# A streaming encoder layer on one core: another order of the products in the input projection, and weight sums of the up projection kept in DRAM

## The chip, the core and the metric

The kernel runs on one core of a Trainium2 chip. A core has five engines that each work through their own queue of instructions in order: TensorE (PE in the profile; it loads a stationary operand, PEld, and streams a moving one through it), VectorE (DVE), ScalarE (ACT), GpSimd (POOL) and SyncE (SP, which here only issues DMAs). They wait for one another by semaphores. Matrix products accumulate in PSUM banks, everything else lies in SBUF, and 16 DMA engines move data between SBUF and DRAM. The metric is the device time of one execution in microseconds (us).

## The reference

One layer over 2048 prompt frames and 8 x 16 sample frames (2176 columns together), model width 1024, in float32:

```
h = rms_norm(x, g_mix_pre)
qa, ka, va, qb, kb, vb, ga, gb = split(h @ w_in)        # w_in: 1024 x 4352
qa, ka = rope(qa), rope(ka)
oa = sliding-window attention with sinks (qa, ka, va)
ob = chunk-band attention with relative bias (qb, kb, vb)
mixed = sigmoid(ga) * (oa @ w_oa) + sigmoid(gb) * (ob @ w_ob)
x = x + rms_norm(mixed @ w_out, g_mix_post)
u, val = split(rms_norm(x, g_ffn_pre) @ w_up)           # w_up: 1024 x 5632
conv = conv_b + causal depthwise convolution of u, 3 taps
x = x + rms_norm((gelu(conv) * val) @ w_down, g_ffn_post)
```

The outputs are x of both parts, new rows of the caches, and the last two rows of u.

## The kernel before

The stages follow one another: input projection (to about 860 us), attention (to 1500), output projection (to 1757), up projection (to 2763), down projection. The change touches the first and the fourth.

**A float32 product from three.** Every operand is split into a high part (`hi`, a cast on ACT, L143) and the rest (`lo`, a subtraction on DVE, L144), and `mm3` runs three matmuls for each 128 rows of depth: hi by xhi (L138), hi by xlo (L139), lo by xhi (L140).

**Seven products for eight.** Two output tiles of 128 rows and two column ranges of n columns are made together from seven products instead of eight (the Strassen-Winograd form), each of 4 x 3 matmuls; the sums of weights and of inputs that it needs are made beforehand. `seven` issues the products in the order of a table of (product, bank), three PSUM banks in all: products 1 and 2 add up in bank 0; 6, 7 and 4 in bank 1; 5 and 3 in bank 2. Banks are read between the products: s1 is a copy of bank 0 after product 1 (ACT), q is bank 1 + s1 after product 6 (DVE), and product 7 adds to bank 1 only when q has been read; t is bank 1 + s1 after product 7, and product 4 waits for that; product 2 waits for s1.

**Input projection.** After four output tiles that are made directly come 41 "pairs" of tiles: 15 in a first block of columns, 17 in a second (n = 384 in both), 9 in a third (n = 320). In the first two blocks, pairs of queries, keys and values take turns with pairs of gates. Queries and keys get a rotary step on ACT and DVE (L331 to L352) and go to DRAM as hi and lo. For a pair, `in_place` loads two raw weight tiles (`wraw`, `wrow`, 512 KB each), splits `wraw` (products 1 and 2) and half of `wrow` (`whib`, `wlob`: product 4), lets POOL make four sums in the same tiles (L257 to L260), and splits the sums: `wrow` for products 7 and 5, `wraw` again as `whic`, `wloc` for products 6 and 3. It is called for the next pair before the present one is issued.

**Up projection.** Three blocks of columns, 22 units each (66 in all; n = 364, 364, 360). `stationary` loads two raw tiles per unit, POOL writes four sums to a tile `ws` (one buffer; L193 to L196), and they are split like the others. `up` runs the seven products (order 1, 6, 5, 7, 2, 4, 3), then the convolution, the gelu and the product, and stores `gd` (L1229). At the start of a block, `moving` makes the sums and splits of the block's x: DVE (L1081, L1083), POOL (L1087, L1090), and seven splits `x1h`, `x1l` and so on.

**What sets the order.** The code states what depends on what; a list scheduler, which estimates when each operation can run, then sets the order of instructions in each engine's queue. An operation that is issued earlier in the program has the higher priority. An instruction that waits holds up all that is behind it on its engine.

Of the kernel before, what the change touches and what calls it, by code (L numbers as in the profile page):

```python
# [10 lines left out]
F32 = mybir.dt.float32  # L11
# [6 lines left out]
P = 128  # L18
# [8 lines left out]
NF = FF // P  # L27
# [26 lines left out]
ORDER = ((1, 0), (6, 1), (5, 2), (7, 1), (2, 0), (4, 1), (3, 2))  # L54

IBLOCKS = [(0, 384), (768, 384), (1536, 320)]
IORDER = ((1, 0), (5, 2), (6, 1), (7, 1), (2, 0), (4, 1), (3, 2))
IW = 384
DIRECT = 4
LATES = ((1536, 320), (1856, 320))  # L60
# [37 lines left out]
def encoder_layer(ctx: ExitStack, tc: tile.TileContext, i, o):  # L98
# [17 lines left out]
    md = [dram.tile([P, T], F32, name=f"md{p}") for p in range(8)]  # L116
    xd = [dram.tile([P, T], F32, name=f"xd{p}") for p in range(8)]
    extd = dram.tile([8, NT, EXT], F32, name="extd")
    gd = [dram.tile([P, T], F32, name=f"gd{f}") for f in range(NF)]


# [60 lines left out]
    wp = Weights(ctx.enter_context(tc.tile_pool(name="wraw", bufs=2)),  # L182
                 ctx.enter_context(tc.tile_pool(name="whl", bufs=3)))

    def stationary(src0, src1, wx, sx):

        r0 = wp.raw.tile([P, 8, P], F32, name="wraw")
        r1 = wp.raw.tile([P, 8, P], F32, name="wraw")
        dma(out=r0, in_=src0)
        dma(out=r1, in_=src1)  # L190
        sums = sx.tile([P, 16, P], F32, name="ws")
        s1, s2, s3, s4 = [sums[:, 4 * z:4 * z + 4] for z in range(4)]
        G.tensor_add(out=s1, in0=r1[:, 0:4], in1=r1[:, 4:8])  # L193
        G.tensor_sub(out=s2, in0=s1, in1=r0[:, 0:4])  # L194
        G.tensor_sub(out=s3, in0=r0[:, 0:4], in1=r1[:, 0:4])  # L195
        G.tensor_sub(out=s4, in0=r0[:, 4:8], in1=s2)  # L196
        w = {}

        def put(pool, tag, src, names):
            nk = 4 * len(names)  # L200
            hi = pool.tile([P, nk, P], F32R, name=f"whi{tag}", tag=f"whi{tag}")
            lo = pool.tile([P, nk, P], F32R, name=f"wlo{tag}", tag=f"wlo{tag}")
            split(hi, lo, src)
            for z, name in enumerate(names):
                w[name] = (hi[:, 4 * z:4 * z + 4], lo[:, 4 * z:4 * z + 4])

        put(wp.hl, "", r0, (1, 2))
        put(wx, "b", r1[:, 4:8], (4,))
        put(wp.hl, "", sums[:, 0:8], (5, 6))
        put(wx, "c", sums[:, 8:16], (7, 3))  # L210
        return w

    def seven(w, x, n, evac, bank_pool, order):

        ps = [bank_pool.tile([P, 512], F32, name="psm3")[:, :n] for _ in range(3)]
        began = set()
        for z, (name, bank) in enumerate(order):
            (whi, wlo), (xhi, xlo) = w[name], x[name]
            for k in range(4):
                mm3(ps[bank], whi[:, k], wlo[:, k], xhi[:, k], xlo[:, k],  # L220
                    k == 0 and bank not in began, k == 3, bank in began)
            began.add(bank)
            evac(z, ps)
# [4 lines left out]
    with ExitStack() as ph:  # L228
# [9 lines left out]
        def in_place(src0, src1):  # L238

            r0 = wp.raw.tile([P, 8, P], F32, name="wraw")  # L240
            r1 = wr.tile([P, 8, P], F32, name="wrow")
            dma(out=r0, in_=src0)
            dma(out=r1, in_=src1)
            a11, a12, a21, a22 = r0[:, 0:4], r0[:, 4:8], r1[:, 0:4], r1[:, 4:8]
            w = {}

            def put(pool, tag, src, names):
                nk = 4 * len(names)
                hi = pool.tile([P, nk, P], F32R, name=f"whi{tag}", tag=f"whi{tag}")
                lo = pool.tile([P, nk, P], F32R, name=f"wlo{tag}", tag=f"wlo{tag}")  # L250
                split(hi, lo, src)
                for z, name in enumerate(names):
                    w[name] = (hi[:, 4 * z:4 * z + 4], lo[:, 4 * z:4 * z + 4])

            put(wp.hl, "", r0, (1, 2))
            put(wx, "b", a22, (4,))
            G.tensor_add(out=a22, in0=a21, in1=a22)  # L257
            G.tensor_sub(out=a21, in0=a11, in1=a21)
            G.tensor_sub(out=a11, in0=a22, in1=a11)
            G.tensor_sub(out=a12, in0=a12, in1=a11)  # L260
            put(wp.hl, "", r1, (7, 5))
            put(wx, "c", r0, (6, 3))
            return w

        def segments(t0, n):

# [182 lines left out]
            put(3, b22)  # L449
            yield x  # L450

        def pair(u, bi, w, x):
            b0, n = IBLOCKS[bi]
            ta, tb = b0, b0 + n
            s1, q, t = [ev.tile([P, IW], F32, name=z)[:, :n] for z in ("s1", "q", "t")]

            def tile_f():
                return ev.tile([P, IW], F32, name="f", bufs=4)[:, :n]

            def ready(z, ps):  # L460
                if z == 0:
                    S.copy(out=s1, in_=ps[0])  # L462
                elif z == 2:
                    V.tensor_add(out=q, in0=ps[1], in1=s1)
                elif z == 3:
                    V.tensor_add(out=t, in0=ps[1], in1=s1)  # L466
                    f = tile_f()
                    V.tensor_add(out=f, in0=ps[2], in1=t)
                    evac(u + 1, tb, n, f)
                elif z == 4:  # L470
                    f = tile_f()
                    S.copy(out=f, in_=ps[0])
                    evac(u, ta, n, f)
                elif z == 5:
                    f = tile_f()
                    V.tensor_add(out=f, in0=ps[1], in1=s1)
                    evac(u + 1, ta, n, f)
                elif z == 6:
                    f = tile_f()
                    V.tensor_add(out=f, in0=ps[2], in1=q)  # L480
                    evac(u, tb, n, f)

            seven(w, x, n, ready, psm, IORDER)

        hp2 = [None]

# [66 lines left out]
            units += [(bi, u) for u in turns]  # L553
        weights = lambda u: in_place(i["w1"][u], i["w1"][u + 1])
        ws = [weights(units[0][1])]
        for x in xgen:
            pass
        nxt = iter(())
        seen = 0
        for z, (bi, u) in enumerate(units):  # L560
# [14 lines left out]
                nxt = iter(())  # L575
            if z + 1 < len(units):
                ws.append(weights(units[z + 1][1]))
            if bi < 2 and u == 20:
                nxt = stage(bi + 1)
            hs = next(nxt, hs)  # L580
            pair(u, bi, ws.pop(0), x)
        late.update({g: (x[y], x[y2]) for g, y, y2 in ((0, 1, 2), (1, 0, 3))})
    xr.close()

# [589 lines left out]
    with ExitStack() as ph:  # L1174
# [11 lines left out]
        def up(bi, f, w, x):  # L1186
# [21 lines left out]
                elif z == 6:  # L1208
                    V.tensor_add(out=u1, in0=ps[2], in1=q)

            seven(w, x, n, evac, psm, ORDER)
            cv = sp.tile([P, NBK], F32, name="cv", bufs=2)[:, :nb]
            S.activation(out=cv, in_=ue[:, 2:2 + nb], func=AF.Identity, bias=cw[:, f, 3:4], scale=cw[:, f, 2:3])
            V.tensor_copy(out=hist[:, f], in_=ue[:, npr:npr + 2])
# [14 lines left out]
            dma(out=gd[f][:, b0:b0 + nb], in_=cv)  # L1229

        units = [(bi, f) for bi in range(3) for f in range(NF)]
        ws = [stationary(i["wu"][f], i["wu"][NF + f], wx, sx) for _, f in units[:1]]
        x = None
        for z, (bi, f) in enumerate(units):
            if f == 0:
                if bi:
                    xgen = moving(hs, SBLOCKS[bi][1], hq, lambda: hx)
                for x in xgen:
                    pass
            if z + 1 < len(units):  # L1240
                g = units[z + 1][1]
                ws.append(stationary(i["wu"][g], i["wu"][NF + g], wx, sx))
            if f == 16 and bi < 2:
                hs = stage(bi + 1)
            up(bi, f, ws.pop(0), x)
# [149 lines left out]
```

## Time and profile before

| | us |
|---|---|
| median of 3 runs (lowest, highest) | 3318.76 (3317.17, 3323.16) |
| profiled execution, whole | 3322.67 |
| profiled execution, span of the trace | 3320.6 |
| PE, DVE, ACT, POOL busy | 3069.1, 2187.1, 1483.7, 776.4 |
| input projection, 50 to 840 us: PE waits for q, for s1 | 39.7, 27.4 |
| up projection, busy time of POOL's four sums (66 units) | 92.9 + 112.1 + 95.5 + 127.1 |

The profile is of one execution, so the rows below have one duration for each instruction. Busy time of PE includes matmuls at either level of its clock (1.2 and 2.4 GHz); PEclk is the mean granted clock of a window as a share of the upper one. The idle time before an instruction stands in brackets with what released it. Names are those of the program, without buffer numbers (`s` is s1, `psm` a PSUM bank of a pair or unit).

### The profile page before, as it was taken

Reading aid. Unit: us, or ns where it says so; the run is one execution under the profiler, and the core shown is the slowest. Engines: PE = TensorE matmul, PEld = TensorE weight load, DVE = VectorE, ACT = ScalarE, POOL = GpSimd, SP = SyncE. Lnnn points to the kernel's source line nnn. Section 1 sums busy time; section 2 is a strip of 40 time slices with the busy share of each in tenths; the row PEclk is TensorE's granted clock in tenths of the full one; section 3 lists DMA queues with packets and bytes.
Section 4 is the critical chain, followed back from the end, with each engine's and each line's share of the span. In section 5 each row is a group of like instructions: output and inputs, shape, how many; then the busy total and the mean of one; then the engine's idle time right before and its main releaser. Section 6 shows DMA issues by size and latency. Waiting matters only on the chain.

```text
span 3320.6 us, 49296 instructions
## 1 busy us (share of the span) xinstructions
PE 3069.1 (92%) x18188; PEld 2833.1 (85%) x18188; DVE 2187.1 (66%) x3632; ACT 1483.7 (45%) x2647; POOL 776.4 (23%) x612
## 2 busy tenths in 40 slices
PE   6888898977799999999997999899989999999997
PEld 5788788876787777789996999799989998888897
DVE  7755657456347766554688877987787775445445
ACT  5544445344238766313444444444444444433432
POOL 2233432332111111000003444444444440000000
PEclk8999999988999999999998999999999999999999
DMA  4543445435676663674534222322222226556554
GB/s 137 167 139 110 136 130 149 137 97 157 201 249 193 178 166 113 199 223 155 162 115 140 98 97 103 117 103 97 100 85 101 103 98 204 168 163 201 158 177 148
DMA packets 276666, 479.14 MB, mean 144 GB/s; under 512 B 33729, under 2 KB 171337, under 8 KB 276425
## 3 DMA queue, kind: packets, MB, share of 16 engines
q1 hardware_dynamic: 272328, 462.36, 45.0%
q0 software_dynamic: 4096, 13.64, 1.2%
q8 instruction: 143, 2.34, 0.3%
q14 instruction: 99, 0.80, 0.1%
HBM read 360.71 MB, written 115.15 MB: 143 GB/s over the span
## 4 chain that ended last, share of the span: by engine, by line
PE 57%; DVE 8%; POOL 5%; issue 3%; ACT 2%; DMA 2%; SPq 0%; POOLq 0%; DVEq 0%; ACTq 0%
PE psm L138 14%; PE psm L140 14%; PE psm L139 14%; PE pso L908 4%; PE pst L925 3%; PE pss L863 2%; DVE wlo L144 2%; POOL ws L194 1%; DVE cv L1216 1%; POOL ws L196 1%; POOL ws L193 1%; PE pss L839 1%; POOL ws L195 1%; ACT whi L143 1%; PE psf L138 1%
## 5 line engine op out<-in xcount | busy, mean ns | idle before, releaser
L144 DVE TENSOR_TENSOR wlo<-wraw,whi 128x1024 fp32r<-128x1024 f32 (+1 forms) x259 | 346.5, 1339 | 374.9 <-ACT whi L143 371.4
L143 ACT CAST whi<-wraw 128x1024 fp32r<-128x1024 f32 (+1 forms) x259 | 263.2, 1017 | 547.8 <-PE psm L139 452.8
L138 PE MATMUL psm<-ghl,whi 128*128 128x464 f32 (+1 forms) x880 | 320.4, 364 | 2.7 <-ACT ghl L143 2.2
L139 PE MATMUL psm<-ghl,whi 128*128 128x464 f32 (+1 forms) x880 | 317.7, 361 | 2.0 <-DVE ghl L144 2.0
L140 PE MATMUL psm<-ghl,wlo 128*128 128x464 f32 (+1 forms) x880 | 317.0, 360 | 1.0 <-DVE wlo L144 1.0
L193 POOL TENSOR_TENSOR ws<-wraw 128x512 f32<-128x512 f32 x66 | 92.9, 1407 | 566.3 <-DVE wlo L144 449.0
L138 PEld LDWEIGHTS psm<-ghl,whi 128*128 128x128 f32 x880 | 165.8, 189 | 20.9 <-ACT ghl L143 3.3
L140 PEld LDWEIGHTS psm<-ghl,wlo 128*128 128x128 f32 x880 | 165.9, 189 | 18.4 <-DVE wlo L144 1.6
L139 PEld LDWEIGHTS psm<-ghl,whi 128*128 128x128 f32 x880 | 166.3, 189 | 18.0 <-DVE ghl L144 2.8
L138 PE MATMUL psm<-x2h,whi 128*128 128x364 f32 (+3 forms) x428 | 150.3, 351 | 33.6 <-ACT s L462 30.4
L138 PE MATMUL psm<-x5h,whi 128*128 128x364 f32 (+3 forms) x428 | 144.4, 337 | 26.1 <-ACT whi L143 9.8
L257 POOL TENSOR_TENSOR wrow<-wrow 128x512 f32<-128x512 f32 x41 | 57.9, 1412 | 469.1 <-DVE wlob L144 436.4
L138 PE MATMUL psm<-x4h,whib 128*128 128x364 f32 (+3 forms) x428 | 145.1, 339 | 18.6 <-DVE t L466 12.3
L138 PE MATMUL psm<-x3h,whic 128*128 128x364 f32 (+3 forms) x428 | 143.0, 334 | 10.1 <-DVE vv L1203 7.2
L139 PE MATMUL psm<-x2l,whi 128*128 128x364 f32 (+3 forms) x428 | 147.3, 344 | 4.1 <-DVE x2l L144 4.1
L138 PE MATMUL psm<-mhi,whi 128*128 128x272 f32 x512 | 150.7, 294 | 0.0
L140 PE MATMUL psm<-mhi,wlo 128*128 128x272 f32 x512 | 148.1, 289 | 0.0
L139 PE MATMUL psm<-mlo,whi 128*128 128x272 f32 x512 | 147.5, 288 | 0.0
L138 PE MATMUL psm<-x1h,whi 128*128 128x364 f32 (+3 forms) x428 | 144.2, 337 | 2.8 <-ACT x1h L143 1.3
L140 PE MATMUL psm<-x2h,wlo 128*128 128x364 f32 (+3 forms) x428 | 146.1, 341 | 0.0
L139 PE MATMUL psm<-x5l,whi 128*128 128x364 f32 (+3 forms) x428 | 143.0, 334 | 2.5 <-DVE x5l L144 2.5
L140 PE MATMUL psm<-x1h,wlo 128*128 128x364 f32 (+3 forms) x428 | 143.8, 336 | 1.7 <-DVE wlo L144 1.7
(368 smaller groups left out, 9599.1 us busy)
## 6 DMA issues: line engine op xcount, KB each, us to landing
wraw<-in_wu SPq DMA_DIRECT2D x132, 512.0 KB, 4.1
wraw<-in_wd SPq DMA_DIRECT2D x80, 512.0 KB, 3.7
wraw<-in_w SPq DMA_DIRECT2D x69, 512.0 KB, 3.8
wrow<-in_w SPq DMA_DIRECT2D x41, 512.0 KB, 3.9
keys<-kd SPq DMA_DIRECT2D x80, 256.0 KB, 4.3
gx<-gd SPq DMA_DIRECT2D x88, 232.0 KB, 4.0
q<-qd SPq DMA_DIRECT2D x64, 256.0 KB, 4.2
gd<-cv SPq DMA_DIRECT2D x44, 364.0 KB, 2.3
```

The source lines that it names most:

```text
L138: TE.matmul(ps, lhsT=hi, rhs=xhi, start=first, stop=False, skip_group_check=more)
L139: TE.matmul(ps, lhsT=hi, rhs=xlo, start=False, stop=False, skip_group_check=more)
L140: TE.matmul(ps, lhsT=lo, rhs=xhi, start=False, stop=last, skip_group_check=more)
L143: S.copy(out=hi, in_=src)
L144: E.tensor_sub(out=lo, in0=src, in1=hi.bitcast(F32))
L193: G.tensor_add(out=s1, in0=r1[:, 0:4], in1=r1[:, 4:8])
L194: G.tensor_sub(out=s2, in0=s1, in1=r0[:, 0:4])
L195: G.tensor_sub(out=s3, in0=r0[:, 0:4], in1=r1[:, 0:4])
L257: G.tensor_add(out=a22, in0=a21, in1=a22)
L863: TE.matmul(ps[:, off + n0:off + n1], lhsT=q[:, j * P:(j + 1) * P], rhs=keys[hf][:, z, k0 + n0:k0 + n1], start=(z == 0), stop=(z == 1))
L908: TE.matmul(ps_o[hf * HD:(hf + 1) * HD, q0 * P:(q0 + nq) * P], lhsT=v[:, hf * HD:(hf + 1) * HD], rhs=tsb[hf][:, col:col + nq * P], start=( ...
L925: TE.transpose(out=tp[:, col:col + P], in_=u["P"][hf][j][:, bl * P:(bl + 1) * P], identity=ident)
```

## The change

Three edits. The input projection takes its products in the table `ORDER`, as the up projection does: 1, 6, 5, 7, 2, 4, 3 instead of 1, 5, 6, 7, 2, 4, 3, and q is taken after the second product. `in_place` becomes a generator: its first part (loads, first splits, sums) runs before the pair as it did, its last two splits are issued within the pair after its fifth product. In the up projection, block 1 also stores the tile of sums to DRAM (`sd`, 1 MB for each of 22 units); blocks 2 and 3 load it instead of making it, and load only half of the second raw tile.

```diff
-IORDER = ((1, 0), (5, 2), (6, 1), (7, 1), (2, 0), (4, 1), (3, 2))
...
+    sd = [dram.tile([P, 16, P], F32, name=f"sd{f}") for f in range(NF)]
...
-    def stationary(src0, src1, wx, sx):
+    def stationary(src0, src1, wx, sx, kept, first):
...
-        dma(out=r1, in_=src1)
+        if first:
+            dma(out=r1, in_=src1)
+        else:
+            dma(out=r1[:, 4:8], in_=src1[:, 4:8])
         sums = sx.tile([P, 16, P], F32, name="ws")
-        s1, s2, s3, s4 = [sums[:, 4 * z:4 * z + 4] for z in range(4)]
-        G.tensor_add(out=s1, in0=r1[:, 0:4], in1=r1[:, 4:8])
-        G.tensor_sub(out=s2, in0=s1, in1=r0[:, 0:4])
-        G.tensor_sub(out=s3, in0=r0[:, 0:4], in1=r1[:, 0:4])
-        G.tensor_sub(out=s4, in0=r0[:, 4:8], in1=s2)
+        if first:
+            s1, s2, s3, s4 = [sums[:, 4 * z:4 * z + 4] for z in range(4)]
+            G.tensor_add(out=s1, in0=r1[:, 0:4], in1=r1[:, 4:8])
+            G.tensor_sub(out=s2, in0=s1, in1=r0[:, 0:4])
+            G.tensor_sub(out=s3, in0=r0[:, 0:4], in1=r1[:, 0:4])
+            G.tensor_sub(out=s4, in0=r0[:, 4:8], in1=s2)
+            dma(out=kept, in_=sums)
+        else:
+            dma(out=sums, in_=kept)
...
-    def seven(w, x, n, evac, bank_pool, order):
+    def seven(w, x, n, evac, bank_pool):
...
-        for z, (name, bank) in enumerate(order):
+        for z, (name, bank) in enumerate(ORDER):
...
             G.tensor_sub(out=a12, in0=a12, in1=a11)
+            yield w
             put(wp.hl, "", r1, (7, 5))
             put(wx, "c", r0, (6, 3))
-            return w
+            yield w
...
-        def pair(u, bi, w, x):
+        def pair(u, bi, w, x, ahead):
...
-                elif z == 2:
+                elif z == 1:
                     V.tensor_add(out=q, in0=ps[1], in1=s1)
...
                     S.copy(out=f, in_=ps[0])
+                    next(ahead, 0)
                     evac(u, ta, n, f)
...
         ws = [weights(units[0][1])]
+        w = next(ws[0])
+        next(ws[0])
...
                 ws.append(weights(units[z + 1][1]))
+                nw = next(ws[-1])
...
-            pair(u, bi, ws.pop(0), x)
+            pair(u, bi, w, x, ws[-1])
+            w = nw
...
-                ws.append(stationary(i["wu"][g], i["wu"][NF + g], wx, sx))
+                ws.append(stationary(i["wu"][g], i["wu"][NF + g], wx, sx, sd[g], units[z + 1][0] == 0))
```

What the scheduler makes of it is shown at three places. PE first, in pair 6 of the first block (pairs counted from 0). Before, from the end of product 6 (`x6h`) over the beginning of product 2 (`x2h`) to the beginning of product 7 (`x7h`):

```order
L139 MATMUL psm_1893<-x6l,whic 128x384
L140 MATMUL psm_1893<-x6h,wloc 128x384
L138 MATMUL psm_1892<-x2h,whi 128x384
L139 MATMUL psm_1892<-x2l,whi 128x384
L140 MATMUL psm_1892<-x2h,wlo 128x384
L138 MATMUL psm_1892<-x2h,whi 128x384
L139 MATMUL psm_1892<-x2l,whi 128x384
L138 MATMUL psm_1893<-x7h,whi 128x384
L139 MATMUL psm_1893<-x7l,whi 128x384
```

After, from the end of product 5 (`x5h`), which now follows product 6, to the beginning of product 7:

```order
L138 MATMUL psm_1908<-x5h,whi 128x384
L139 MATMUL psm_1908<-x5l,whi 128x384
L140 MATMUL psm_1908<-x5h,wlo 128x384
L138 MATMUL psm_1907<-x7h,whi 128x384
L139 MATMUL psm_1907<-x7l,whi 128x384
L140 MATMUL psm_1907<-x7h,wlo 128x384
L138 MATMUL psm_1907<-x7h,whi 128x384
```

Five matmuls of product 2 stood between product 6 and product 7; now all of product 5 stands there, and product 2 follows product 7.

DVE in the same pair. `psm_1893` before and `psm_1907` after are bank 1 of the pair; `wloc` belongs to the next pair's weights. Before:

```order
L144 TENSOR_TENSOR wlob<-wrow,whib 128x512
L352 SCALAR_TENSOR_TENSOR lo<-f,hi 128x384
L480 TENSOR_TENSOR f<-psm_1756,q 128x384
L144 TENSOR_TENSOR wloc<-wraw,whic 128x1024
L464 TENSOR_TENSOR q<-psm_1893,s_1889 128x384
L466 TENSOR_TENSOR t<-psm_1893,s_1889 128x384
L468 TENSOR_TENSOR f<-psm_1894,t 128x384
```

After (q is now L472, t is L474, f L476):

```order
L360 SCALAR_TENSOR_TENSOR lo<-f,hi 128x384
L144 TENSOR_TENSOR wlob<-wrow,whib 128x512
L489 TENSOR_TENSOR f<-psm_1770,q 128x384
L472 TENSOR_TENSOR q<-psm_1907,s_1903 128x384
L144 TENSOR_TENSOR wloc<-wraw,whic 128x1024
L474 TENSOR_TENSOR t<-psm_1907,s_1903 128x384
L476 TENSOR_TENSOR f<-psm_1908,t 128x384
```

q and `wloc` have changed places here. Over the 40 pairs that have a next one, q now stands ahead of the next pair's `wloc` in 14 (1 to 6, 12, 15, 16, 22, 24, 25, 35 and 36) and behind it in 26; before it stood behind it in about 34.

POOL at the start of block 2 of the up projection, whose sums for x are L1087 and L1090 before and L1100 and L1103 after. Before:

```order
L196 TENSOR_TENSOR ws<-wraw,ws 128x512
L1087 TENSOR_TENSOR hst<-hst 128x4x364
L193 TENSOR_TENSOR ws<-wraw 128x512
L195 TENSOR_TENSOR ws<-wraw 128x512
L194 TENSOR_TENSOR ws<-ws,wraw 128x512
L196 TENSOR_TENSOR ws<-wraw,ws 128x512
L1090 TENSOR_TENSOR xt<-hst,xt 128x1456
L193 TENSOR_TENSOR ws<-wraw 128x512
```

After, from the last weight sums of block 1 over the starts of blocks 2 and 3:

```order
L197 TENSOR_TENSOR ws<-wraw 128x512
L199 TENSOR_TENSOR ws<-wraw 128x512
L198 TENSOR_TENSOR ws<-ws,wraw 128x512
L200 TENSOR_TENSOR ws<-wraw,ws 128x512
L1100 TENSOR_TENSOR hst<-hst 128x4x364
L1103 TENSOR_TENSOR xt<-hst,xt 128x1456
L1100 TENSOR_TENSOR hst<-hst 128x4x360
L1103 TENSOR_TENSOR xt<-hst,xt 128x4x360
```

Four weight sums stood between the two x sums of a block; after the change POOL has nothing but the x sums in blocks 2 and 3.

## Rows read from the trace of the kernel before

**Rows 1.** The page's first part: busy us, share of the span, instructions.

```profile
PE 3069.1 (92%) x18188; PEld 2833.1 (85%) x18188; DVE 2187.1 (66%) x3632; ACT 1483.7 (45%) x2647; POOL 776.4 (23%) x612
```

**Rows 2.** Busy time by windows; last three columns: clock, DMA share, GB/s.

```profile
52.00:215.00 163.00, 124.86 (x610) 118.36 (x609) 109.33 (x138) 81.72 (x123) 55.98 (x36) 0.86 0.50 142
2095.00:2187.00 92.00, 76.22 (x422) 72.92 (x421) 83.85 (x89) 38.98 (x47) 45.67 (x22) 0.94 0.31 110
2187.00:2430.00 243.00, 242.74 (x1450) 242.44 (x1450) 194.65 (x242) 110.19 (x139) 102.31 (x69) 1.00 0.28 102
2430.00:2519.00 89.00, 76.12 (x427) 73.06 (x426) 75.63 (x100) 38.14 (x47) 44.79 (x24) 0.94 0.22 81
```

**Rows 3.** Waits of PE, 50 to 840 us: total, times, longest, in us.

```profile
PE psm L138 <- DVE q L464: 39.7, 29, 4.8
PE psm L138 <- ACT s L462: 27.4, 23, 2.9
```

**Rows 4.** Timeline, pairs 0 and 6: start, duration, engine, [idle before, releaser].

```profile
87.60 0.55 DVE L464 TENSOR_TENSOR q<-psm,s 128x384 f32<-128x384 f32 x1
200.28 0.34 PE L139 MATMUL psm<-x2l,whi 128*128 128x384 f32 x1
201.43 1.04 ACT L143 CAST whic<-wraw 128x1024 fp32r<-128x1024 f32 x1 [4.58 <-POOL wraw L260]
202.51 1.23 DVE L144 TENSOR_TENSOR wloc<-wraw,whic 128x1024 fp32r<-128x1024 f32 x1 [4.31 <-ACT whic L143]
203.65 0.55 DVE L464 TENSOR_TENSOR q<-psm,s 128x384 f32<-128x384 f32 x1
204.26 0.44 PE L138 MATMUL psm<-x7h,whi 128*128 128x384 f32 x1 [3.64 <-DVE q L464]
205.57 0.52 PE L138 MATMUL psm<-x7h,whi 128*128 128x384 f32 x1
```

**Rows 5.** Timeline, a later pair of block 1, at the same place.

```profile
444.10 0.33 PE L139 MATMUL psm<-x6l,whic 128*128 128x384 f32 x1
444.27 0.34 PE L140 MATMUL psm<-x6h,wloc 128*128 128x384 f32 x1
444.30 1.23 DVE L144 TENSOR_TENSOR wloc<-wraw,whic 128x1024 fp32r<-128x1024 f32 x1 [5.34 <-ACT whic L143]
445.44 0.55 DVE L464 TENSOR_TENSOR q<-psm,s 128x384 f32<-128x384 f32 x1
446.05 0.44 PE L138 MATMUL psm<-x7h,whi 128*128 128x384 f32 x1 [0.21 <-DVE q L464]
```

**Rows 6.** Timeline at the start of block 2 of the up projection.

```profile
2097.76 4.25 POOL L1087 TENSOR_TENSOR hst<-hst 128x1456 f32<-128x1456 f32 x1 [8.77 <-DVE hst L1081]
2099.18 4.36 DVE L1083 TENSOR_TENSOR xt<-hst 128x1456 f32<-128x1456 f32 x1
2106.58 2.32 DVE L144 TENSOR_TENSOR x6l<-xt,x6h 128x1456 fp32r<-128x1456 f32 x1
2112.70 3.26 POOL L1090 TENSOR_TENSOR xt<-hst,xt 128x1456 f32<-128x1456 f32 x1
2115.99 1.41 ACT L143 CAST x4h<-xt 128x1456 fp32r<-128x1456 f32 x1 [5.56 <-POOL xt L1090]
2119.34 0.67 PE L138 MATMUL psm<-x6h,whi 128*128 128x364 f32 x1 [6.12 <-ACT whi L143]
```

**Rows 7.** Timeline: POOL in a steady unit of block 2, stores of block 3.

```profile
2315.66 1.30 POOL L193 TENSOR_TENSOR ws<-wraw 128x512 f32<-128x512 f32 x1 [8.04 <-DVE wlo L144]
2319.54 2.15 POOL L196 TENSOR_TENSOR ws<-wraw,ws 128x512 f32<-128x512 f32 x1
2529.86 0.33 SPq L1229 DMA_DIRECT2D gd<-cv  x1
2742.80 0.33 SPq L1229 DMA_DIRECT2D gd<-cv  x1
```

**Rows 8.** The page's DMA issues: count, KB each, median us to landing.

```profile
wraw<-in_wu SPq DMA_DIRECT2D x132, 512.0 KB, 4.1
```

More of the change, by code (lines that the diff above doesn't have):

```diff
@@ L481, in ready @@
                     evac(u, tb, n, f)
-            seven(w, x, n, ready, psm, IORDER)
+            seven(w, x, n, ready, psm)
         hp2 = [None]
@@ L1209, in evac @@
                     V.tensor_add(out=u1, in0=ps[2], in1=q)
-            seven(w, x, n, evac, psm, ORDER)
+            seven(w, x, n, evac, psm)
             cv = sp.tile([P, NBK], F32, name="cv", bufs=2)[:, :nb]
@@ L1231, in encoder_layer @@
         units = [(bi, f) for bi in range(3) for f in range(NF)]
-        ws = [stationary(i["wu"][f], i["wu"][NF + f], wx, sx) for _, f in units[:1]]
+        ws = [stationary(i["wu"][f], i["wu"][NF + f], wx, sx, sd[f], True) for _, f in units[:1]]
         x = None
```

## The prediction

> **What bounds the kernel now.** I began with the engines' shares: TensorE (PE) is busy for 92% of the span, VectorE (DVE) for 66%, ScalarE (ACT) for 45%, GpSimd (POOL) for 23% [rows 1]. So the change can only pay where PE stands still or runs at the lower clock, and the busy time by windows says where that is. In the middle of the up projection's block 2 PE is busy 242.74 of 243 us at a clock of 1.00; at the starts of its blocks 2 and 3 it is idle for 15.8 of 92 us and 12.9 of 89 us; in the first pairs of the input projection it is busy 124.86 of 163 us at a mean clock of 0.86 [rows 2]. POOL sums taken from the steady up units free an engine that bounds nothing there; they count at the block starts.
>
> The waits of PE in the input projection come next: two waits lead, on q (39.7 us, 29 times) and on s (27.4 us, 23 times) [rows 3]. The timeline shows why both are late. Queues are in order, and the next pair's weights stand in front: ACT's cast `whic` waits for POOL's sums, DVE's `wloc` waits for `whic`, and DVE's q waits behind `wloc`. In an early pair, `whic` starts at 201.43, `wloc` runs from 202.51, q from 203.65, and PE, which had started its last matmul at 200.28, goes on at 204.26 after 3.64 us of nothing; then its matmuls last 0.52 us, where they took 0.34 before: the clock has dropped from 2.4 to 1.2 GHz [rows 4]. In a later pair the same queue costs less: product 6 starts its last matmul at 444.27, q starts at 445.44, product 7 at 446.05 [rows 5].
>
> **Part one: order of the products.** Before, PE runs 1, 5, 6, then five matmuls of 2, then 7. After, it runs 1, 6, 5, 7, 2, 4, 3. At full clock a matmul takes 0.17 us (444.10 to 444.27 [rows 5]), a product of twelve 2.08 us and a pair of 84 14.5 us. q now has product 5 as cover, 2.08 us, but loses the five matmuls of 2, 0.87 us, and it is needed 2.08 us earlier counted from product 1. So the change helps where q can be issued on time, and hurts where q still stands behind `wloc`.
>
> The changed order on DVE decides which. q now stands ahead of `wloc` in pairs 1 to 6 of block 0 and in eight later ones (counting pairs from 0), and still behind it in 26 of 40.
>
> Pairs 1 to 6: from q of pair 0 at 87.60 to q of pair 6 at 203.65 are six pairs of 19.3 us [rows 4], 4.8 over the 14.5 of pure matmuls. The q wait goes, and with it the half-clock stretch behind it. But I do not give back all 4.8: DVE is busy for 109.33 of the 163 us [rows 2], that is 15 us for each of the 7.3 pairs' worth of matmuls recorded there (610/84), so the splits, the rotary steps and their stores become late next. I take 16.5 us a pair: 6 x 2.8 = 17 us. Bounds: 0 (evacuation bounds these pairs at 19.3 anyway) and 6 x 4.8 = 29.
>
> The eight later pairs with q in front: of the 67.1 us of q and s waits [rows 3], about 20 lie in pairs 1 to 6 (up to 3.64 each [rows 4]). The other 47 spread over 34 pairs; eight of them at the mean have 11 us, and with a little half clock behind the longest I take 12 (bounds 5 and 20).
>
> The pairs still blocked: q is ready when `wloc` is done, whatever PE does in between. In [rows 5] PE was ready for product 7 at 444.27 + 0.17 = 444.44, and it began at 446.05: 1.6 us, of which five matmuls of 2 filled 0.87. After the change nothing fills it, and those five run later. 26 pairs are in this case by the order, 7 of which lie near block starts or the tail, where PE waits for other things anyway; 19 x 0.87 = 16.5, I take a loss of 16 us. Bounds: a loss of 26 x 0.87 = 23, and 0, because the late issue of the splits also puts s ahead of `whic` more often (before, `whic` came first in 24 of 40 pairs, after in 16 to 18).
>
> The late issue itself (the splits `put` after product 2) adds no instruction; it moves priorities, and its effect is the order just counted. SP's loads for a pair stay ahead of it. Input projection: -17 - 12 + 16 = -13 us.
>
> **Part two: sums kept in DRAM.** Of 66 x 4 POOL sums, 44 x 4 go. In exchange block 1 writes 22 x 1 MB, and blocks 2 and 3 read 44 x 1 MB less the 44 x 0.25 MB of the second row that is left out: 33 MB more.
>
> *Block starts.* At the start of block 2, POOL does its first stage sum at 2097.76, then four weight sums, then the second stage sum from 2112.70 to 2115.96; `x4h` on ACT waits for that until 2115.99; two casts later PE resumes at 2119.34, after 6.12 us of nothing [rows 6]. Block 3 does the same. After the change POOL's two stage sums stand next to each other, 10.7 us sooner. What is late next is DVE: splits of the new x (2.32 us each here, beside POOL [rows 6]). The two windows hold 15.8 + 12.9 = 28.7 us of idle PE [rows 2]; I take half, 14 us. Bounds: 0 (DVE's splits bound it alone) and 29.
>
> Here the trace has DVE's L1083 at 4.36 us, begun while POOL's L1087 (4.25 us) was running, and ended 1.5 us after it [rows 6]. The Trainium skill, SBUF — State Buffer, "Who interferes with whom", says that a DVE instruction with two SBUF inputs and a GpSimd instruction that reads SBUF share a port, and that the later one is blocked for the whole of the first. The trace agrees. By that rule L1083 stays at about 4.4 us, since L1087 stays beside it, and the 2 us that PE waits behind it stay too; had the weight sums been what slows it, the term would be 14 + 2 x 2.3 = 18.6. The half that I take needs neither.
>
> *Block 3's steady units.* The stores of gd at 2529.86 and 2742.80 are 15 units apart: 14.20 us each. Scaled by 360/364 columns from the 0.1674 us of a matmul in block 2 (242.74/1450 [rows 2]) a unit of 84 is 13.91 us [rows 7]. I put the 0.29 us down to q behind `wloc`, as in the input projection; without POOL's sums in front `whic` can start sooner. 15 x 0.29 = 4 us gained, bounds 0 and 6.
>
> *Is the load of the sums on time?* The buffer `ws` is free when POOL starts its next sums, 2315.66, and they end at 2319.54 + 2.15 = 2321.69 [rows 7]. A load issued at 2315.6 has 6.1 us to be no later. Two raw loads of 512 KB, issued together, land in 4.1 us [rows 8], so 1 MB should land at about 2319.8. I cost it at 0; bounds below.
>
> *Block 1.* The write of `ws` holds the only `ws` buffer until it has landed, and stands in SP's queue before the next unit's loads. By the same 4.1 us it ends well inside a unit of 14 us, but at the block's start, where loads pile up, I take a loss of 3 us (bounds 0, and 22 x 1 = 22 if each write puts one raw load late by 1 us).
>
> Up projection: -14 - 4 + 3 = -15 us.
>
> **Sum.** -13 - 15 = -28 us. The profiled execution took 3322.67 us, 2.1 over its span, and 3.9 over the median of the runs, 3318.76; no term hangs on that difference, so I take the sum from the median: 3318.76 - 28 = 3291 us.
>
> **Rivals.**
> *Slower: stalls that bring the clock down.* The still blocked pairs stall for 1.6 us with nothing in between. After 3.64 us the clock fell [rows 4]. The 1.6 us of [rows 5] were half filled by matmuls of 2 and say nothing of an empty stall of that length. If it brings the clock down, product 7 runs at 1.2 GHz, 12 x 0.16 = 1.9 us more. Over 19 pairs this is +36, so 3327; over all 26, with their extra 0.87 for the other seven, +55, so 3346. Middle 3336. Against it: a stall must repeat at this size, and many are shorter. Chance 0.10.
> *Slower or even: late loads.* PE is never late on these sums in block 2 (242.74 of 243 us [rows 2]), so the load decides from a landing somewhat over 6.1 us after its issue; from there each us is paid in up to 42 units, and 1 us past it the time is 3291 + 42 = 3333. For it: it queues behind the gd store and in one queue with the raw loads. Against: the DMA engines are busy only 28% of that stretch [rows 2]. Chance 0.04.
> *No change.* Evacuation keeps pairs 1 to 6 at 19.3 (0 instead of -17), the other stage-1 terms cancel (-12 + 16), and the block starts give only a third: 3318.76 + 4 - 10 + 3 - 4 = 3312; with block starts giving nothing, 3322. Between them, about 3317. Chance 0.14.
> *Better.* Pairs 1 to 6 reach 15 us (-26), blocked pairs lose nothing, block starts give 24: -26 - 12 - 24 - 4 + 3 = -63: 3256. Chance 0.12.
> *My forecast*, 0.60, with its own range 3273 to 3308.
>
> **The numbers.** Range 3260 to 3319: the lower end takes in nearly all of the forecast and most of the better case; the upper end takes half of the no-change case and leaves out the two slower ones (0.14). Runs can tell about 0.2%, 6.6 us. Faster than 3312.1: 0.60 + 0.12 + 0.05 = 0.77. Within: 0.09, nearly all from the no-change case. Slower: 0.14.
>
> **What would show it.** In the changed profile: the q wait of the input projection well under 39.7 us in pairs 1 to 6 and their spacing 16 to 17 us; the s wait smaller; q waits of 1 to 1.7 us in pairs like that of [rows 5] with the clock after them at 0.34 us a matmul (at 0.52 the first rival holds); POOL without weight sums at the starts of blocks 2 and 3 and no 6-us wait on `x4h`; a unit of 13.9 to 14.0 us in block 3. I am wrong if pairs 1 to 6 stay near 19 us, if a wait for the load of `ws` appears in blocks 2 and 3, or if the clock of the input projection falls below what it is now.

## The result and the profile after

The changed kernel takes 3294.72 us in the median of 4 runs (3290.96 to 3296.18), the kernel before 3317.97 us on the same chip (4 runs): a ratio of 0.9929, 95% interval 0.9910 to 0.9948, so 0.7% faster. The forecast was 3291 us. The profiled executions differ by more than the medians, 3292.1 against 3320.6 us of span; the parts below are read from these two and add up to 28.5 us, not to the 23 of the medians.

First the page's busy times, as in [rows 1]:

```profile
PE 3049.7 (93%) x18188; PEld 2829.8 (86%) x18188; DVE 2121.1 (64%) x3632; ACT 1484.0 (45%) x2645; POOL 489.9 (15%) x436
```

POOL has lost 286.5 us, ten times what the span has: that engine bounded nothing over most of it. PE's own busy time is 19 us less for the same 18188 matmuls, which points to fewer of them at the lower clock.

Where the time went, by one event at each place (q is its start on DVE, the end of a unit is the start of its last matmul, of product 3; both read from the timelines of the two kernels):

| point | before | after | difference |
|---|---|---|---|
| q of pair 6 | 203.65 | 186.88 | -16.8 |
| q of the last pair (40) | 846.59 | 833.84 | -12.8 |
| up projection, unit 0 ends | 1793.64 | 1782.53 | -11.1 |
| unit 20 (late in block 1) | 2088.38 | 2086.97 | -1.4 |
| unit 25 (block 2 has started) | 2180.47 | 2168.04 | -12.4 |
| unit 42 | 2419.49 | 2406.87 | -12.6 |
| unit 47 (block 3 has started) | 2507.94 | 2488.00 | -19.9 |
| unit 65, the last | 2763.12 | 2737.00 | -26.1 |
| end of the span | 3320.6 | 3292.1 | -28.5 |

So the early pairs win 16.8 us and the other pairs give 4.0 back; block 1 of the up projection gives 9.7 back; the starts of blocks 2 and 3 win 11.0 and 7.3; block 3's units win 6.2. Of block 1's 9.7 us, 2.9 are lost by unit 4 and 6.8 in the steady units 4 to 20.

The windows that answer to [rows 2] (each begins and ends at the same work as there; columns as there):

```profile
52.00:198.00 146.00, 112.54 (x606) 108.09 (x605) 107.90 (x138) 81.32 (x123) 53.90 (x36) 0.92 0.57 157
2093.00:2175.00 82.00, 75.21 (x428) 74.02 (x427) 72.91 (x89) 40.25 (x47) 7.59 (x2) 0.96 0.49 171
2187.00:2406.00 219.00, 219.00 (x1310) 219.00 (x1309) 152.25 (x217) 97.84 (x125) 0.00 (x0) 1.00 0.46 159
2417.00:2499.00 82.00, 73.81 (x428) 72.30 (x427) 66.67 (x100) 38.78 (x47) 6.28 (x2) 0.96 0.41 140
```

In the early pairs the clock is 0.92 where it was 0.86. At the block starts PE is idle for 6.8 and 8.2 us where it was 15.8 and 12.9, and POOL has two instructions left in each. Then the waits of PE in the input projection, as in [rows 3]:

```profile
PE psm L138 <- DVE q L472: 60.8, 29, 5.0
PE psm L138 <- ACT s L470: 9.7, 5, 3.2
```

The wait on s is down from 27.4 to 9.7 us, but the one on q is up from 39.7 to 60.8, in the same number of places. Two pairs show both sides. Pair 6, which stood still for 3.64 us in [rows 4]:

```profile
186.88 0.56 DVE L472 TENSOR_TENSOR q<-psm,s 128x384 f32<-128x384 f32 x1 [3.06 <-PE psm L140]
188.53 0.33 PE L140 MATMUL psm<-x5h,wlo 128*128 128x384 f32 x1
188.71 0.33 PE L138 MATMUL psm<-x7h,whi 128*128 128x384 f32 x1
188.86 1.05 ACT L143 CAST whic<-wraw 128x1024 fp32r<-128x1024 f32 x1 [3.64 <-POOL wraw L267]
189.95 1.23 DVE L144 TENSOR_TENSOR wloc<-wraw,whic 128x1024 fp32r<-128x1024 f32 x1 [2.51 <-ACT whic L143]
```

q runs at 186.88, 3 us ahead of `wloc`, and product 7 (188.71) follows product 5 without a gap. A pair of the second block, where the scheduler left `wloc` in front, as in [rows 5]:

```profile
578.56 1.05 ACT L143 CAST whic<-wraw 128x1024 fp32r<-128x1024 f32 x1 [3.73 <-POOL wraw L267]
579.58 0.34 PE L140 MATMUL psm<-x5h,wlo 128*128 128x384 f32 x1
579.65 1.23 DVE L144 TENSOR_TENSOR wloc<-wraw,whic 128x1024 fp32r<-128x1024 f32 x1 [5.38 <-ACT whic L143]
580.79 0.55 DVE L472 TENSOR_TENSOR q<-psm,s 128x384 f32<-128x384 f32 x1
581.39 0.44 PE L138 MATMUL psm<-x7h,whi 128*128 128x384 f32 x1 [1.48 <-DVE q L472]
583.43 0.33 PE L140 MATMUL psm<-x7h,wlo 128*128 128x384 f32 x1
```

PE has finished product 5 soon after 579.58, `wloc` starts at 579.65, q behind it at 580.79, product 7 at 581.39: 1.6 us of nothing, as computed, and the matmuls behind it still take 0.33 us. Nine stalls before product 7 are 1.3 to 1.8 us long in this trace; behind eight of them the matmuls keep that length. Behind the ninth they do not, and the granted clock from 614.32 to 616.00 is 0.59:

```profile
614.32 0.44 PE L138 MATMUL psm<-x7h,whi 128*128 128x384 f32 x1 [1.78 <-DVE q L472]
615.19 0.52 PE L138 MATMUL psm<-x7h,whi 128*128 128x384 f32 x1
```

Of the twelve stalls of more than 2 us before product 7, eleven have matmuls at the lower clock within that product.

The start of block 2, as in [rows 6]:

```profile
2095.90 4.25 POOL L1100 TENSOR_TENSOR hst<-hst 128x1456 f32<-128x1456 f32 x1 [21.63 <-DVE hst L1094]
2097.32 4.37 DVE L1096 TENSOR_TENSOR xt<-hst 128x1456 f32<-128x1456 f32 x1
2104.09 1.66 DVE L144 TENSOR_TENSOR x6l<-xt,x6h 128x1456 fp32r<-128x1456 f32 x1
2105.83 3.34 POOL L1103 TENSOR_TENSOR xt<-hst,xt 128x1456 f32<-128x1456 f32 x1 [5.67 <-DVE x6l L144]
2106.16 4.53 DVE L144 TENSOR_TENSOR x7l<-hst,x7h 128x1456 fp32r<-128x1456 f32 x1
2109.20 1.41 ACT L143 CAST x4h<-xt 128x1456 fp32r<-128x1456 f32 x1 [0.66 <-POOL xt L1103]
2112.56 0.44 PE L138 MATMUL psm<-x6h,whi 128*128 128x364 f32 x1 [0.73 <-ACT whi L143]
2119.31 0.43 PE L140 MATMUL psm<-x1h,wlo 128*128 128x364 f32 x1 [3.78 <-DVE wlo L144]
```

`x4h` waits for nothing long (POOL's second sum starts at 2105.83 instead of 2112.70), and PE's wait of 6.12 us is 0.73. `x6l` takes 1.66 us instead of 2.32. L1096, which was L1083, still takes 4.37 us beside L1100, and `x7l` now takes 4.53 beside L1103. The wait of product 3 for DVE stays as well (2.28 us, at 2102.19; 2.27 before). PE stands still later instead, 3.78 us at 2119.31, for the split `wlo` of a weight that DVE reaches only after all the splits of x. The stores of block 3 that answer to [rows 7], 13 units apart:

```profile
2508.31 0.33 SPq L1242 DMA_DIRECT2D gd<-cv  x1
2688.14 0.33 SPq L1242 DMA_DIRECT2D gd<-cv  x1
```

A unit there takes 13.83 us, where it took 14.20, and PE has no wait left; before, its weight load for product 7 waited for q in 16 units between 2519 and 2763 us (6.3 us in all).

### The profile page after: what moved, and what is told of

It is laid out like the page before. It is cut to its first block, busy times and chain, and to the rows that moved or that the text cites. A ratio compares the mean times of both kernels' runs of the same rounds, so it can differ in the third digit from the quotient of the medians.

```text
span 3292.1 us, 49253 instructions
## 1 busy us (share of the span) xinstructions
PE 3049.7 (93%) x18188; PEld 2829.8 (86%) x18188; DVE 2121.1 (64%) x3632; ACT 1484.0 (45%) x2645; POOL 489.9 (15%) x436
## 4 chain that ended last, share of the span: by engine, by line
PE 61%; issue 6%; POOL 6%; DMA 5%; DVE 5%; ACT 2%; SPq 1%; POOLq 0%; DVEq 0%; ACTq 0%
PE psm L138 15%; PE psm L140 15%; PE psm L139 15%; PE pso L921 4%; DMA wraw<-in_wu 3%; PE pst L938 3%; PE pss L876 2%; POOL ws L198 1%; PE pss L852 1%; POOL ws L200 1%; PE psf L138 1%; POOL ws L199 1%; POOL ws L197 1%; PE psf L139 1%; PE psf L140 1%
## 5 line engine op out<-in xcount | busy, mean ns | idle before, releaser
L144 DVE TENSOR_TENSOR wlo<-wraw,whi 128x1024 fp32r<-128x1024 f32 (+1 forms) x259 | 313.2, 1211 | 380.6 <-ACT whi L143 374.1
L139 PE MATMUL psm<-x1l,whi 128*128 128x364 f32 (+3 forms) x428 | 143.1, 334 | 1.7 <-DVE x1l L144 1.7
L139 PE MATMUL psm<-x4l,whib 128*128 128x364 f32 (+3 forms) x428 | 143.4, 335 | 0.0
L140 PE MATMUL psm<-x4h,wlob 128*128 128x364 f32 (+3 forms) x428 | 143.2, 335 | 0.0
```

The costliest lines, as they stand in the source:

```text
L139: TE.matmul(ps, lhsT=hi, rhs=xlo, start=False, stop=False, skip_group_check=more)
L140: TE.matmul(ps, lhsT=lo, rhs=xhi, start=False, stop=last, skip_group_check=more)
L144: E.tensor_sub(out=lo, in0=src, in1=hi.bitcast(F32))
```

## The experiments

All were timed in 5 rounds, beside the kernel before on the same chip; "against before" is by the ratio of the runs.

**The input projection's order alone.** In the kernel before:

```diff
-                elif z == 2:
+                elif z == 1:
                     V.tensor_add(out=q, in0=ps[1], in1=s1)
...
-            seven(w, x, n, ready, psm, IORDER)
+            seven(w, x, n, ready, psm, ORDER)
```

> The kernel before with the new product order in the input projection and q taken after the second product; splits of the weight sums issued where they were, up projection as before. Theory A (the order is what pays in the input projection, the late issue adds next to nothing): about 10 us under the kernel before, q of pair 6 some 15 us earlier than in the kernel before, q waits of 1.4 to 1.9 us in most pairs of the second block. Theory B (the late issue pays, the order alone costs, since q loses the five matmuls of product 2 in front of it): the same time as before or up to 10 us more.

Measured: 3308.95 us, ratio 0.9969 (0.9958 to 0.9980), 10 us under before; q of pair 6 at 187.58, 16 us sooner than before. Theory A's number.

**The late issue alone**: the generator and the call within the pair, products in the old order, up projection as before (the first lines against the kernel before, the last against the changed kernel).

```diff
                     S.copy(out=f, in_=ps[0])
+                    next(ahead, 0)
                     evac(u, ta, n, f)
...
-            seven(w, x, n, ready, psm)
+            seven(w, x, n, ready, psm, IORDER)
```

> The kernel before with the late issue of the last two splits alone; products in the old order, up projection as before. Theory A: within 4 us of the kernel before, since on DVE q stands ahead of wloc in 7 pairs instead of 5. Theory B: 8 to 12 us under the kernel before, since s stands ahead of whic on ScalarE in 25 pairs instead of 16.

Measured: 3311.65 us, ratio 0.9979 (0.9971 to 0.9988), 7 us under before: between the two expectations, and not the nothing of theory A. Its waits of PE, in the same window:

```profile
PE psm L139 <- DVE q L473: 51.1, 31, 4.8
PE psm L139 <- ACT s L471: 16.3, 15, 2.8
```

s is waited for 16.3 us instead of 27.4, q 51.1 instead of 39.7: s in front of `whic` alone moves the wait from one to the other, with the same total. Still, q of pair 6 comes 9 us sooner than before.

**Both edits of the input projection**: the changed kernel with the up projection as before:

```diff
+        first = True
         if first:
             dma(out=r1, in_=src1)
...
-            dma(out=kept, in_=sums)
```

> The changed kernel with the up projection as before: both edits of the input projection. If the two add up (10.3 for the order and 7.0 for the late issue, each by itself): 17 us under the kernel before. If the late issue only does what the order has done already (s1 and q ahead of the next splits in much the same pairs): 7 to 11 us under it.

Measured: 3305.2 us, ratio 0.9964 (0.9951 to 0.9977), 12 us under before (8 to 16). That is the order's 10 us within the intervals; the sum of 17 lies just outside this run's interval, but the terms of that sum have intervals of their own, so the times alone do not decide. The queues do: with the order alone q stands ahead of the next `wloc` in 15 pairs and s ahead of the next `whic` in 21, with both edits in 14 and 22. Beside the new order the late issue changes next to nothing in them.

**The up projection's part alone**, with the input projection of the kernel before (`stationary` as in the change):

```diff
-                ws.append(stationary(i["wu"][g], i["wu"][NF + g], wx, sx))
+                ws.append(stationary(i["wu"][g], i["wu"][NF + g], wx, sx, sd[g], units[z + 1][0] == 0))
```

> The kernel before with the stored sums in the up projection alone. Theory A (the parts add up; read from the changed kernel's trace: 10 us lost in block 1, 11 won at the start of block 2, 7 at the start of block 3, 6 in block 3's units, 2 in the down projection): 15 to 18 us under the kernel before. Rival (the up stage's gain is owed to its earlier or other start behind the new input projection): under 8 us.

Measured: 3303.2 us, ratio 0.9952 (0.9940 to 0.9965), 16 us under before: the expected sum. Units 4 to 20 of block 1 take 231.3 us (1865.09 to 2096.41) where they took 225.0: the loss in block 1 belongs to this part.

**q first everywhere.** To the changed kernel, an order of issue: the next pair's last splits stand behind this pair's s1 on ACT and behind its q on DVE, in all 40 pairs.

```diff
-                    S.copy(out=s1, in_=ps[0])
+                    mark.append(S.copy(out=s1, in_=ps[0]))
...
-                    V.tensor_add(out=q, in0=ps[1], in1=s1)
+                    mark.append(V.tensor_add(out=q, in0=ps[1], in1=s1))
...
-                    next(ahead, 0)
+                    with tc.issue_after(mark[0].ins), tc.issue_after(mark[1].ins):
+                        next(ahead, 0)
```

> The changed kernel with the next pair's last two splits forced behind s1 on ScalarE and behind q on VectorE in every pair (the order of issue alone). Theory A (whic and wloc standing in front of s1 and q make the 1.4 to 1.9 us stalls between products 5 and 7): the q waits of 61 us in the input projection fall under 20, and the time is 25 to 40 us under the changed kernel. Rival (the next pair's weights are needed as early as they stand now, or evacuation sets the pace): PE waits as long elsewhere, mostly for wloc before product 6, and the time is within 5 us of the changed kernel or above it.

Measured: 3241.7 us, ratio to before 0.9767 (0.9753 to 0.9781): 53 us under the changed kernel, more than the 25 to 40 expected. The waits on q:

```profile
PE psm L138 <- DVE q L474: 30.5, 11, 5.4
```

11 times instead of 29; 30.5 us stay, above the 20 expected. PE waits for `wloc` only 2.6 us in all, so the rival falls. From q of pair 6 to q of pair 40 the kernel is 50.6 us shorter than the changed one: 39.8 us of it is PE's idle time, the rest busy time, at a clock of 0.95 instead of 0.93. A pair of the second block:

```profile
556.78 0.48 ACT L472 COPY s<-psm 128x384 f32<-128x384 f32 x1 [3.23 <-PE psm L140]
558.92 0.56 DVE L474 TENSOR_TENSOR q<-psm,s 128x384 f32<-128x384 f32 x1 [2.87 <-PE psm L140]
559.51 1.05 ACT L143 CAST whic<-wraw 128x1024 fp32r<-128x1024 f32 x1 [2.25 <-POOL wraw L267]
560.57 0.34 PE L140 MATMUL psm<-x5h,wlo 128*128 128x384 f32 x1
560.59 1.22 DVE L144 TENSOR_TENSOR wloc<-wraw,whic 128x1024 fp32r<-128x1024 f32 x1 [1.12 <-ACT whic L143]
560.74 0.33 PE L138 MATMUL psm<-x7h,whi 128*128 128x384 f32 x1
```

s at 556.78, q at 558.92, and only then `whic` and `wloc`, for which PE does not wait here; product 7 follows product 5 at once. From this q at 558.92 to the third after it (602.60) a pair takes 14.56 us, 84 x 0.173. So where the stall is gone, it was the queue's order. Ten stalls of over 1 us before product 7 are left. In three of them, of 3.1 to 5.4 us, the timeline shows q behind other work on DVE once more: in two behind the staging of the next block's x (L404), in the third behind a split of that x, which had itself waited for ACT. The one before product 7 at 514.27, 3.12 us:

```profile
506.63 7.12 DVE L404 SCALAR_TENSOR_TENSOR hst<-hst,gv,r 128x640 f32<-128x640 f32 x4
513.67 0.55 DVE L474 TENSOR_TENSOR q<-psm,s 128x384 f32<-128x384 f32 x1
```

**The old order with q first**: the same edit of the changed kernel, with products in the order 1, 5, 6, 7, 2, 4, 3 and q taken after the third.

```diff
-                elif z == 1:
+                elif z == 2:
                     mark.append(V.tensor_add(out=q, in0=ps[1], in1=s1))
...
-            seven(w, x, n, ready, psm)
+            seven(w, x, n, ready, psm, IORDER)
```

> The changed kernel with q and s1 forced ahead of the next pair's last splits, but with the old order of products (1, 5, 6, 7, 2, 4, 3; q after the third). Theory A (product 5 between 6 and 7 is worth something only as cover for q, and five matmuls of product 2 cover most of it): steady pairs of 14.6 to 15.1 us against 14.56 with the new order, 0 to 20 us above it in all, so 3242 to 3262. Rival (the order itself is what gains): stalls of 0.5 us or more at q in nearly every pair, and 3270 or more.

Measured: 3252.58 us, ratio 0.9805 (0.9792 to 0.9818). Against 0.9767 for the new order this is 0.38%, 13 us, inside theory A's 0 to 20. PE's waits on q are these:

```profile
PE psm L139 <- DVE q L475: 35.7, 18, 4.8
```

Beside the up projection's part alone (0.9952) the queue is worth 1.5% here, 49 us, with the old order of products (the late issue among it); the new order is worth 13 us more once the queue is right.

**The store behind the next loads.** To the changed kernel: on SP each store of the sums is issued after the next unit's raw loads.

```diff
-            dma(out=kept, in_=sums)
+            held.append((kept, sums))
...
-            dma(out=r1, in_=src1)
+            d1 = dma(out=r1, in_=src1)
...
+        if held:
+            with tc.issue_after(d1.ins):
+                dma(out=held[0][0], in_=held.pop()[1])
```

> The changed kernel with each store of the sums queued behind the next unit's raw loads on SyncE. Theory A (in block 1 the 1 MB store goes first and holds up the raw loads, which land in some 6 to 8 us instead of 4.1): raw loads land in about 4 us again, units of block 1 take 14.06 us again, and the time is 5 to 9 us under the changed kernel. Rival (the store delays through DMA time in all, or through the single buffer of sums): block 1 keeps its 10 us of loss, the time stays within 3 us.

Measured: 3311.1 us, ratio 0.9981 (0.9972 to 0.9990): 16 us slower than the changed kernel. Theory A fell, and the rival's 3 us were too few, though the single buffer that it names is what the trace shows. The raw loads did land sooner, as the DMA issues of 1870 to 2090 us show, for the changed kernel and for this one (count, KB, median us to landing):

```profile
sd<-ws SPq DMA_DIRECT2D x15, 1024.0 KB, 4.9
wraw<-in_wu SPq DMA_DIRECT2D x30, 512.0 KB, 6.2
```

```profile
sd<-ws SPq DMA_DIRECT2D x15, 1024.0 KB, 7.9
wraw<-in_wu SPq DMA_DIRECT2D x29, 512.0 KB, 4.2
```

But POOL's first sum of a unit waits for something else now. Its waits in the same window, in the changed kernel (with SP's wait before it issues the store) and in this one (the first sum of each unit; total, times, longest):

```profile
POOL ws L197 <- DMA wraw<-in_wu: 104.0, 13, 9.1
SPq L201 <- POOL ws L200: 120.4, 15, 9.3
```

```profile
POOL ws L202 <- DMA sd<-ws: 107.9, 12, 9.9
```

In this kernel's timeline, the sums end at 1930.71 + 1.63, the loads go out, then the store; the next sums start when the store has landed:

```profile
1930.71 1.63 POOL L205 TENSOR_TENSOR ws<-wraw,ws 128x512 f32<-128x512 f32 x1
1932.36 0.33 SPq L191 DMA_DIRECT2D wraw<-in_wu  x1
1933.22 0.42 SPq L198 DMA_DIRECT2D sd<-ws  x1
1941.70 1.30 POOL L202 TENSOR_TENSOR ws<-wraw 128x512 f32<-128x512 f32 x1 [9.37 <-DMA sd<-ws]
```

There is one buffer of sums, and the store must have left it before POOL may write the next. Either way 2 MB go between one unit's sums and the next: 1932.34 to 1941.70 is 9.4 us, and with POOL's 6.5 us (1925.86 to 1932.34) the loop is longer than a unit of 14.06 us. In the changed kernel the loop closes over the raw loads: SP holds the store until POOL's last sum is made, the loads go behind the store, and the next sums wait for them. 104.0/13 = 8.0 us of waiting and 6.5 of sums make 14.5, and (2086.97 - 1855.20)/16 = 14.49 us is what a unit took from unit 4 to 20. Here it closes over the store: 107.9/12 + 6.5 = 15.5, and the units took 15.35.

PE meets the loop at q. A unit of block 1 in the changed kernel, where `whic` had waited 4.04 us for POOL's last sum:

```profile
1945.99 1.23 DVE L144 TENSOR_TENSOR wloc<-ws,whic 128x1024 fp32r<-128x1024 f32 x1 [2.45 <-ACT whic L143]
1949.03 0.53 DVE L1213 TENSOR_TENSOR q<-psm,s 128x364 f32<-128x364 f32 x1
1949.61 0.43 PE L138 MATMUL psm<-x7h,whic 128*128 128x364 f32 x1 [1.23 <-DVE q L1213]
```

Here too q stands on DVE behind a split of the next unit's weights, and product 7 behind q. Putting q first in the up projection, or a second buffer of sums, was not tried.

**The same with q first in the input projection**, both edits as above (no other line):

```diff
+                    with tc.issue_after(mark[0].ins), tc.issue_after(mark[1].ins):
...
+            held.append((kept, sums))
```

> The changed kernel with q and s1 forced ahead of the next pair's last splits and with the stores of the sums behind the next raw loads. If the two causes are separate: 3241.7 less the 5 to 9 us, 3233 to 3237. If the faster input projection hid or made part of the loss: 3238 to 3242.

Measured: 3260.58 us, ratio 0.9827 (0.9813 to 0.9841), 0.6% or 20 us above the 0.9767 of q first alone: neither expectation. It repeats the last one: the loss is in the up projection and the same behind another input projection.

**Half of the sums kept.** From that loop, fewer bytes should do: only the first two sums are stored and loaded (0.5 MB), POOL makes the other two in all blocks.

```diff
+        dma(out=r1, in_=src1)
...
-            dma(out=kept, in_=sums)
+            dma(out=kept, in_=sums[:, 0:8])
...
-            dma(out=sums, in_=kept)
+            dma(out=sums[:, 0:8], in_=kept)
+        G.tensor_sub(out=s3, in0=r0[:, 0:4], in1=r1[:, 0:4])
+        G.tensor_sub(out=s4, in0=r0[:, 4:8], in1=s2)
```

> The changed kernel with only the first two sums stored (0.5 MB a unit) and loaded; GpSimd makes the other two in all three blocks, and both raw tiles are loaded whole. Theory C (from the changed kernel and the run with the later store: in block 1 four sums of 6.6 us, then 2 MB of transfers of about 8 us, then the next sums make a loop of 14.6 us, longer than a unit of 14.06): the loop shrinks by the 0.5 MB, some 1.5 to 2 us, below a unit, block 1 loses 5 us less or better, raw loads land in 5 us or less; the starts of blocks 2 and 3 lose 0 to 4 us each, block 3's units stay at 13.83. Time 0 to 8 us under the changed kernel. Rival (any store on SyncE ahead of the raw loads costs that): block 1's units stay at 14.1 to 15.8.

Measured: 3289.77 us, ratio 0.9911 (0.9897 to 0.9924), against 0.9929 (0.9910 to 0.9948): the medians are 5 us apart, the intervals overlap. The trace is plainer than the time. DMA issues and POOL's first wait in block 1:

```profile
wraw<-in_wu SPq DMA_DIRECT2D x30, 512.0 KB, 3.9
sd<-ws SPq DMA_DIRECT2D x14, 512.0 KB, 2.6
```

```profile
POOL ws L194 <- DVE wlo L144: 112.6, 14, 8.0
```

Raw loads land in 3.9 us again, and POOL waits for DVE, as it did in the kernel before, and no longer for a transfer. Units 4 to 20 take 224.96 us (1850.27 to 2075.23), to the hundredth what they took before. Two things are changed at once, though: the store is half as large, and it goes out before the last sum is made, 2.2 us ahead of the raw loads (at 1904.92, the first load at 1907.15) where it stood right before them. Which of the two frees the loads is not shown. The start of block 2 (units 20 to 25) takes 85.5 us, against 92.1 before and 81.1 with all sums loaded; block 3's units stay at 13.83 us.

**Half kept, and q first**: both edits together.

```diff
+                    with tc.issue_after(mark[0].ins), tc.issue_after(mark[1].ins):
...
+            dma(out=kept, in_=sums[:, 0:8])
```

> The same with q and s1 forced ahead of the next pair's last splits in the input projection. Theory C and separate causes: 3241.7 less 0 to 8 us, 3234 to 3242. Rival: above 3242.

Measured: 3237.81 us, ratio 0.9758 (0.9745 to 0.9772), the fastest of all, 57 us under the changed kernel; its gain over q first alone (0.9767) is within the intervals.

## Why the prediction was right, point by point

*The bound.* Right: PE's idle time and lower clock in the input projection and at the block starts were where the time was, and POOL's 286 us less counted at the block starts and, as the prediction's own term for them says, in block 3's units.

*Pairs 1 to 6, -17.* Right: (186.88 - 86.32)/6 is 16.8 us a pair, where 16.5 was taken and 19.3 stood before. Not every wait went: pair 3 still stands for 4.3 us before product 7.

*The other pairs, -12 and +16.* Their sum, +4, is what the trace shows (-16.8 becomes -12.8), and the mechanism of the loss is in the timeline: stalls of 1.6 us where 0.87 had been filled. The terms were not as large as said: from one start of product 7 to the next, the eight later pairs with q in front won 3.9 us together, and all others from pair 7 on lost 6.7. The first term has a misreading in it: of those eight pairs, four (15, 25, 35 and 36) had q ahead of `wloc` in the kernel before as well, so only four could be freed. So both terms were more than twice too big, and their errors cancelled.

*The late issue, 0.* Right: the prediction counted the queue order that both edits make, and gave the late issue nothing beside it. By itself it is worth 7 us, but beside the new order it leaves the queues nearly as they are.

*Block starts, -14.* Right in kind, too small: -11.0 and -7.3. PE's idle time fell by 13.9 us between the points of the table, the half that was taken; the other 4.5 us is busy time of PE, in windows whose clock went from 0.94 to 0.96, and for that the prediction had no term. The wait behind `x4h` went, and what is late next is DVE, as was said, though its splits take 1.66 us, not 2.32, where POOL is out of their way. That L1083 would stay at 4.4 us beside POOL's sum of x held (4.37), and so did PE's wait behind it (2.28 us before product 3).

*Block 3's units, -4.* -6.2: the whole stall went, 0.34 us in each of 18 units, where 0.29 in 15 was taken. The cause was the one named, PE waiting for q.

*The loads in blocks 2 and 3, 0.* Right: block 2's PE is busy for 219.00 of 219 us.

*Block 1, +3: the step that failed.* It cost 9.7 us. The prediction said that the store "ends well inside a unit of 14 us" and put the loss at the block's start, by the landing time of loads that had the DMA engines to themselves. It did not add up what stands between one unit's sums and the next: store, raw loads and POOL's sums in a row. The loss of the first units, 2.9 us, is about the 3 that was taken; the other 6.8 is that loop in the steady units. The run with the later store shows the loop, which closes over the store there and gets longer; with a store that is smaller and earlier it is short enough to cost nothing from unit 4 to 20.

*Input -13, up -15.* The parts measured alone are -12 and -16; their sum, -28, lies within the interval of the whole (-23; 17 to 30). The up projection's -15 came out of errors that cancelled, too: block 1 lost 6.7 us more than forecast, and the block starts and block 3's units won 6.5 more.

*The rivals.* The clock fell behind one of the nine stalls of about 1.6 us, where the first rival had it fall behind 19 or 26, and over pairs 6 to 40 it is 0.93 before and after. No load of the sums came late in blocks 2 and 3; the early pairs did not stay at 19.3 us. The forecast was luckier than its working in two places: the terms of blocked and freed pairs were both too large and cancelled, and so did block 1's loss and the greater gains behind it.

## What to carry to other kernels

When an engine's queue is in order and a scheduler fills it by estimates, look at what stands in front of the instruction that PE waits for; covering the wait with other work and moving some of the instructions in front of it was worth 12 us here, putting the instruction first in every pair 53 more. When a sum is replaced by a transfer, add up the loop from one use of its buffer to the next, with every transfer and every instruction in it, and compare it with the period of the stage: a transfer's own landing time is not that number.

## What was not expected of the hardware

Two raw loads of 512 KB that landed in 4.1 us by themselves [rows 8] took 6.2 us behind a 1 MB store issued just before them on the same queue, and the store took 4.9 us; with the order turned round the loads took 4.2 and the store 7.9. In these two runs what was issued first was served first, nearly in full, and the other paid.
